# Rotary embedding: the first batch moved in two-row pieces, with sine and cosine tables of its own

## The chip, the cores and the metric

The kernel runs on one core of a Trainium2 chip. A core has five engines that run their own instruction streams: TensorE (PE, matrix products into PSUM), VectorE (DVE), ScalarE (ACT), GpSimd (POOL) and SyncE (SP, which only issues transfers and waits). Sixteen DMA engines move data between the device memory (HBM) and the core's on-chip memory (SBUF, 128 partitions). SP and ACT issue DMAs here, each into a queue of its own; both queues are served by the same sixteen DMA engines. Engines wait for each other through counters called semaphores; a DMA raises its semaphore by 16 when all its parts have landed.

The metric is device time in microseconds (us) for one execution, lower is better. It is given as the median of several executions. The profile is of one further execution, and its span runs from the first to the last instruction.

## The reference

```python
batch, seq, dim, num_heads = 16, 512, 1024, 16      # head_dim 64, half_dim 32
x = x.reshape(batch, seq, num_heads, head_dim)
x1, x2 = x[..., :half_dim], x[..., half_dim:]
cos, sin = cos[None, :, None, :], sin[None, :, None, :]      # each [seq, 32]
rotated = concatenate([x1 * cos - x2 * sin, x1 * sin + x2 * cos], axis=-1)   # float32
```

Every row of 1024 numbers (one position of one batch) is split into 16 heads of 64, and each head's two halves are rotated by the angle of the position. The input has 33.6 MB, the output as much; the tables have 64 KB each.

## The kernel before

**Tiles.** A batch has 512 rows of 4 KB. Four consecutive rows of one batch make a partition's share in a tile of a single batch (`R1 = 4`), eight rows in a tile of two batches (`R2 = 8`, 64 partitions for each batch). There are ten tiles: batches 0 and 1 alone, then six pairs, then batches 14 and 15 alone (line 41). The text calls them t0 to t9: t0 and t1 are the first two batches, t2 to t7 the pairs, t8 and t9 the last two batches. The buffer `x_sb` is a ring of 40 row slots in each partition, so that t0 to t5 are loaded without waiting for anything, and t6 to t9 take slots over from tiles that have been stored. A tile of a single batch moves in pieces of 16 KB for each partition, a pair in pieces of 32 KB.

**One row slot.** A row slot `u` (64 in all) holds one row in each partition, 128 x 1024 numbers. DVE multiplies it by the cosine into PSUM (`mul`, line 293), POOL multiplies the row with its halves swapped by the sine, one half negated, into `t2_sb`, a ring of six (line 257); one row in eight of a pair is multiplied by DVE instead (line 286). The sum is formed in one of two ways: DVE adds both into `x_sb` (`comb`, line 304), or, for the slots marked in `PE2` (three of eight, away from both ends), PE adds the sine product onto PSUM through an identity matrix (line 224) and ACT copies the result into `x_sb` (line 191). PSUM has three slots for this, so DVE's `mul(u)` waits until slot `u - 3` has been added and read.

**Tables.** `stage` receives cosine and sine in the order of a single batch (four rows for each partition). DVE copies the cosine into PSUM (`c1_ps`, line 264), ACT makes the negated and the plain sine (`s1_sb`, lines 182 and 183). For pairs PE rearranges the tables with the matrix `pick` (line 208) into `pair_ps`, and ACT makes `s2_sb` from it (lines 186 and 187).

**Order.** All orders are written out by hand. ACT issues the load of t0, the two table loads, then the loads of t1 to t5 (lines 153 and 174); then it makes `pick` and the sine tables, and after that walks over the slots. In that walk it also issues the later loads, after slot 17, 25 and 33: t6 once the stores of t0 and t1 have landed (`sem_out[0]`), t7 once that of t2 has, t8 and t9 once that of t3 has (lines 192 to 195). ACT is a single stream, so while it waits for such a store, its next copy (line 191) waits too. SP walks over the slots and issues a tile's store when the tile's last slot is finished (line 161). POOL starts when the sine table and t0 are there (lines 250 to 255). Everything goes out with semaphores, and nothing is decided at run time.

Of the kernel before, what the change touches and what calls it, by code (L numbers as in the profile page):

```python
# [6 lines left out]
def bass_split_heads_rope_kernel(  # L7
# [16 lines left out]
    batch, seq, dim = x.shape  # L24
    H = int(num_heads)
    HD = dim // H
    HALF = HD // 2
    P = 128
    R1 = seq // P
    R2 = 2 * R1  # L30
    assert R1 * P == seq and R1 == 4 and batch % 2 == 0

    fp32 = mybir.dt.float32
# [3 lines left out]
    COPY = mybir.ActivationFunctionType.Copy  # L37
# [3 lines left out]
    tiles = [(b, R1 if b in singles else R2) for b in range(batch) if b in singles or b % 2 == 0]  # L41
# [26 lines left out]
    with ExitStack() as stack:  # L68
        x_sb = stack.enter_context(nc.sbuf_tensor([P, RING, H, 2, HALF], fp32))
        t2_sb = stack.enter_context(nc.sbuf_tensor([P, NT2, H, 2, HALF], fp32))  # L70
        stage = stack.enter_context(nc.sbuf_tensor([P, 2, R1 * HALF], fp32))
        s1_sb = stack.enter_context(nc.sbuf_tensor([P, R1, 2, HALF], fp32))
        s2_sb = stack.enter_context(nc.sbuf_tensor([P, R2, 2, HALF], fp32))
        ident = stack.enter_context(nc.sbuf_tensor([P, P], fp32))
# [2 lines left out]
        tab_ps = stack.enter_context(nc.psum_tensor([P, BANK], fp32))  # L77
# [5 lines left out]
        sem_cos = stack.enter_context(nc.semaphore("cos"))  # L83
# [9 lines left out]
        sem_e = stack.enter_context(nc.semaphore("pe"))  # L93
        sem_g = stack.enter_context(nc.semaphore("pick"))
        sem_t = stack.enter_context(nc.semaphore("pairs"))
        sem_a = stack.enter_context(nc.semaphore("act"))

        c1_ps = tab_ps[:, 0:R1 * HALF].rearrange("p (r d) -> p r d", d=HALF)
        v_ps = tab_ps[:, R1 * HALF:R1 * HALF + HD].rearrange("p (t d) -> p t d", d=HALF)

        def c_of(t, r):
            return c1_ps[:, r, :] if tiles[t][1] == R1 else pair_ps[:, r // R1, 0, r % R1, :]

        def s_of(t, r):
            return s1_sb[:, r] if tiles[t][1] == R1 else s2_sb[:, r]

        x1 = x.rearrange("b (s r) d -> b s (r d)", r=R1)
        o1 = out.rearrange("b (s r) h d -> b s (r h d)", r=R1)
# [4 lines left out]
        def in_dram(single, pairs, t):  # L113
            b, n = tiles[t]
            return single[b] if n == R1 else pairs[:, b:b + 2, :]

        def in_sbuf(t):
            b, n = tiles[t]
            k = b * R1 % RING
            return x_sb[:, k:k + n].rearrange("p n h t d -> p (n h t d)")  # L120
# [26 lines left out]

        def stores_of(k):

            return sum(b * R1 // R2 == k for b, _ in tiles)  # L150

        def load(eng, t):
            eng.dma_start(in_sbuf(t), in_dram(x1, x2, t)).then_inc(sem_in[t], 16)  # L153

        def on_sync(sp):
            for u in range(NU):
                t, r, k = where(u)
                if r == tiles[t][1] - 1:
                    wait_added(sp, u)
                    k = u // R2  # L160
                    sp.dma_start(in_dram(o1, o2, t), in_sbuf(t)).then_inc(sem_out[k] if k < EARLY else sem_rest, 16)
            sp.wait_ge(sem_rest, 16 * sum(stores_of(k) for k in range(EARLY, NU // R2)))

        def on_scalar(ae):
            later = {}
            for t, (b, n) in enumerate(tiles):
                if b * R1 + n <= RING:
                    load(ae, t)
                else:

                    later.setdefault((b * R1 - RING) // R2 * R2 + R2 - 1 + LAG, []).append(t)
                if t == 0:
                    for i, (table, sem) in enumerate(((cos, sem_cos), (sin, sem_sin))):
                        ae.dma_start(stage[:, i, :], table.rearrange("(s r) d -> s (r d)", r=R1)).then_inc(sem, 16)  # L174

            ae.wait_ge(sem_i, 2)
            ae.activation(  # L177
                pick[:], ident[:].rearrange("q (s k) -> q k s", k=2)[:, :, :, None].broadcast_to([P, 2, P // 2, 2]), COPY
            ).then_inc(sem_g, 1)
            ae.wait_ge(sem_sin, 16)  # L180
            sv = stage[:, 1, :].rearrange("s (r d) -> s r d", d=HALF)
            ae.activation(s1_sb[:, :, 0, :], sv, COPY, scale=-1.0)  # L182
            ae.activation(s1_sb[:, :, 1, :], sv, COPY).then_inc(sem_s, 1)  # L183
            ae.wait_ge(sem_t, 2)
            s2 = s2_sb[:].rearrange("p (k r) t d -> p k r t d", r=R1)
            ae.activation(s2[:, :, :, 0, :], pair_ps[:, :, 1, :, :], COPY, scale=-1.0)  # L186
            ae.activation(s2[:, :, :, 1, :], pair_ps[:, :, 1, :, :], COPY).then_inc(sem_s, 1)  # L187
            for u in range(NU):
                if PE2[u]:
                    ae.wait_ge(sem_e, n_pe[u])  # L190
                    ae.activation(xs[:, u % RING, :], t1_ps[:, u % NT1, :], COPY).then_inc(sem_a, 1)  # L191
                for t in later.get(u, ()):
                    k = (tiles[t][0] * R1 - RING) // R2
                    ae.wait_ge(sem_out[k], 16 * stores_of(k))
                    load(ae, t)
# [38 lines left out]
        def on_gpsimd(pl):  # L234
            pl.memset(ident[:], 1.0).then_inc(sem_i, 1)  # L235
            pl.wait_ge(sem_i, 1)
            pl.affine_select(  # L237
                out=ident[:],
                in_=ident[:],
                compare_op=mybir.AluOpType.is_equal,  # L240
                fill=0.0,
                base=0,
                pattern=[[-1, P]],
                channel_multiplier=1,
            ).then_inc(sem_i, 1)
            for u in range(NU):
                if V2[u]:
                    continue
                t, r, k = where(u)
                if (t, r) == (0, 0):  # L250
                    pl.wait_ge(sem_s, 1)
                if (t, r) == (2, 0):
                    pl.wait_ge(sem_s, 2)
                if r == 0:
                    pl.wait_ge(sem_in[t], 16)
                wait_t2_free(pl, u)
                pl.tensor_tensor(  # L257
                    t2_sb[:, u % NT2, :, :, :], swapped(k), over_heads(s_of(t, r)), mult
                ).then_inc(sem_p, 1)

        def on_vector(ve):
            ve.memset(zero[:], 0.0).then_inc(sem_z, 1)  # L262
            ve.wait_ge(sem_cos, 16)
            ve.tensor_copy(c1_ps, stage[:, 0, :].rearrange("s (r d) -> s r d", d=HALF)).then_inc(sem_c, 1)  # L264
            ve.wait_ge(sem_c, 1)
            ve.wait_ge(sem_w, NT1 * EH)

            def pair_tables():
                ve.wait_ge(sem_s, 2)
                row = pair_ps[:, V_ROW // R1, 1, V_ROW % R1, :]  # L270
                ve.tensor_scalar_mul(v_ps[:, 0, :], row, -1.0).then_inc(sem_c, 1)
                ve.tensor_copy(v_ps[:, 1, :], row).then_inc(sem_c, 1)

            first_v = V2.index(True)

            def mul(u):
                t, r, k = where(u)
                if r == 0:
                    ve.wait_ge(sem_in[t], 16)
                if (t, r) == (2, 0):  # L280
                    pair_tables()
                if u == first_v:
                    ve.wait_ge(sem_c, 3)
                if V2[u]:
                    wait_t2_free(ve, u)
                    ve.tensor_tensor(t2_sb[:, u % NT2, :, :, :], swapped(k), over_heads(v_ps), mult)  # L286
                if u >= NT1:
                    v = u - NT1
                    if PE2[v]:
                        ve.wait_ge(sem_a, n_pe[v])  # L290
                    else:
                        ve.wait_ge(sem_v, n_comb[v])
                ve.tensor_tensor(  # L293
                    t1_ps[:, u % NT1, :].rearrange("p (h d) -> p h d", d=HALF),
                    x_sb[:, k, :, :, :].rearrange("p h t d -> p (h t) d"),
                    c_of(t, r)[:, None, :].broadcast_to([P, 2 * H, HALF]),
                    mult,
                ).then_inc(sem_m, 1)

            def comb(u):  # L300
                t, r, k = where(u)
                ve.wait_ge(sem_m, u + 1)
                ve.wait_ge(sem_p, n_pool[u])  # L303
                ve.tensor_tensor(  # L304
                    xs[:, k, :],
                    t1_ps[:, u % NT1, :],
                    t2_sb[:, u % NT2, :, :, :].rearrange("p h t d -> p (h t d)"),
                    add,
                ).then_inc(sem_v, 1)

            for u in range(NU + LEAD):
                if u < NU:
                    mul(u)
                if u >= LEAD and not PE2[u - LEAD]:
                    comb(u - LEAD)
# [39 lines left out]
```

## Time and profile before

| | |
|---|---|
| time, median of 3 runs | 161.21 us (161.02 to 161.35) |
| profiled execution, span | 160.3 us |
| DMA: packets, bytes, mean rate | 3170, 67.26 MB, 419 GB/s |
| busy share of the span: POOL, DVE | 84%, 81% |
| busy share of the span: PE, ACT | 45%, 15% |
| POOL's first multiply | starts at 9.85 us |
| issue to landing, load of t0 | 8.0 us |
| issue to landing, store of t0 | 18.6 us |

The time of the profiled execution is known by its span alone; the span is 0.9 us under the median of the runs. A line of a timeline has the start in us, the length in us, the engine, the source line, the operation, what it writes and reads, how often it ran, and in square brackets how long the engine had been idle before it and what ended that. "ACTq" and "SPq" are DMA issues on ACT and SP. The chain is the work that ended last, followed back from the end: start, length, what. In the DMA view a queue's line has its packets, MB, and its packets' share of the time of 16 DMA engines; q10 is the queue of ACT (the loads) and q1 that of SP (the stores). The row "DMA" of the page gives the busy share of the DMA engines in 40 equal slices of the span, in tenths.

### The profile page before, as it was taken

How to read it: one execution, taken by the hardware profiler on the slowest of the kernel's cores; microseconds unless marked ns; L12 is line 12 of the kernel's file. 1: busy time of each engine (PE TensorE's matmuls, PEld its weight loads, DVE VectorE, ACT ScalarE, POOL GpSimd, SP SyncE). 2: the span in 40 equal slices, each digit the busy share in tenths (PEclk: the TensorE clock that was granted, in tenths of full speed). 3: DMA queues.
4: the chain of work that ended last, by engine and by line, in shares of the span. 5: the costliest groups of instructions: out<-in, count | busy, mean ns of one | idle time of the engine just before them, and what ended most of it. 6: DMA issues, size and time to landing. Idle time of an engine off the chain costs nothing.

```text
span 160.3 us, 522 instructions
## 1 busy us (share of the span) xinstructions
PE 72.8 (45%) x94; PEld 24.0 (15%) x94; DVE 130.3 (81%) x117; ACT 24.4 (15%) x27; POOL 134.9 (84%) x64
## 2 busy tenths in 40 slices
PE   6050004478357936660847105489458435850000
PEld 1020002022202211210221002022202111220000
DVE  0069998599989999996999709899889999999500
ACT  0420000203120222022012010201220402040000
POOL 1059999999999999999999999699999999289400
PEclk9955555557755587689687965555555977699555
DMA  5999999999999999999999999999999999999896
GB/s 147 409 441 474 409 450 409 425 429 429 446 429 458 417 411 466 409 433 401 450 433 425 425 409 458 409 433 433 411 429 462 441 417 401 450 441 441 376 450 294
DMA packets 3170, 67.26 MB, mean 419 GB/s; under 512 B 352, under 2 KB 608, under 8 KB 608
## 3 DMA queue, kind: packets, MB, share of 16 engines
q10 hardware_dynamic: 1728, 33.69, 49.6%
q1 hardware_dynamic: 1440, 33.56, 48.9%
q14 instruction: 2, 0.02, 0.0%
HBM read 33.69 MB, written 33.55 MB: 419 GB/s over the span
## 4 chain that ended last, share of the span: by engine, by line
DMA 60%; POOL 13%; DVE 8%; PE 7%; issue 3%; ACT 2%; ACTq 1%; DVEq 0%
DMA x_sb<-in_x_dram 41%; DMA out_dram<-x_sb 18%; POOL t_sb L257 13%; PE t_ps L224 7%; DVE t_ps L293 5%; DVE x_sb L304 3%; ACT x_sb L191 2%; ACTq L153 1%; ACTq L174 1%; DVE t_sb L286 0%; DVEq L303 0%
## 5 line engine op out<-in xcount | busy, mean ns | idle before, releaser
L257 POOL TENSOR_TENSOR t_sb<-x_sb,s_sb 128x1024 f32<-128x1024 f32 x58 | 134.2, 2346 | 14.8 <-ACT s_sb L183 8.5
L224 PE MATMUL t_ps<-t_sb,ident 128*128 128x512 f32 x84 | 68.0, 957 | 63.0 <-DVE t_ps L293 39.2
L293 DVE TENSOR_TENSOR t_ps<-x_sb,pair_ps 128x1024 f32<-128x1024 f32 x48 | 57.7, 1223 | 9.9 <-ACT x_sb L191 9.8
L304 DVE TENSOR_TENSOR x_sb<-t_ps,t_sb 128x1024 f32<-128x1024 f32 x43 | 52.4, 1218 | 2.6 <-POOL t_sb L257 2.6
L224 PEld LDWEIGHTS t_ps<-t_sb,ident 128*128 128x128 f32 x84 | 22.1, 290 | 108.9 <-DVE t_ps L293 74.6
L191 ACT ACTIVATE x_sb<-t_ps 128x1024 f32<-128x1024 f32 x21 | 21.5, 1023 | 109.9 <-PE t_ps L224 96.9
L293 DVE TENSOR_TENSOR t_ps<-x_sb,tab_ps 128x1024 f32<-128x1024 f32 x16 | 19.3, 1222 | 0.1
L286 DVE TENSOR_TENSOR t_sb<-x_sb,tab_ps 128x1024 f32<-128x1024 f32 x6 | 7.3, 1213 | 0.0
L264 DVE COPY tab_ps<-stage 128x128 f32<-128x128 f32 x1 | 0.3, 294 | 7.8 <-DMA stage<-in_cos_dram 7.8
L208 PE MATMUL pair_ps<-stage,pick 128*128 128x256 f32 x4 | 2.0, 667 | 5.4 <-DMA stage<-in_sin_dram 5.4
L201 PE MATMUL t_ps<-zero 128*128 128x512 bf16 x6 | 2.7, 627 | 1.3 <-DVE zero L262 1.3
L208 PEld LDWEIGHTS pair_ps<-stage,pick 128*128 128x128 f32 x4 | 1.2, 324 | 6.4 <-issue 6.3
L177 ACT ACT_TABLE_LOAD x1 | 1.3, 1283 | 5.5 <-issue 5.5
L201 PEld LDWEIGHTS t_ps<-zero 128*128 128x128 bf16 x6 | 0.7, 136 | 2.4 <-DVE zero L262 1.2
L262 DVE MEMSET zero<- 128x256 uint32 x1 | 0.3, 272 | 0.9 <-PEq L337 0.9
L186 ACT ACTIVATE s_sb<-pair_ps 128x256 f32<-128x256 f32 x1 | 0.4, 383 | 1.7 <-PE pair_ps L208 1.7
L182 ACT ACTIVATE s_sb<-stage 128x128 f32<-128x128 f32 x1 | 0.3, 309 | 2.1 <-DMA stage<-in_sin_dram 2.1
L235 POOL MEMSET ident<- 128x128 f32 x1 | 0.2, 204 | 0.3 <-POOLq L337 0.3
L177 ACT ACTIVATE pick<-ident 128x256 f32<-128x256 f32 x1 | 0.4, 416 | 0.0
L187 ACT ACTIVATE s_sb<-pair_ps 128x256 f32<-128x256 f32 x1 | 0.4, 379 | 0.0
L237 POOL TENSOR_SCALAR_AFFINE_SELECT ident<-ident 128x128 f32<-128x128 f32 x1 | 0.3, 292 | 0.1
L337 POOL MEMSET const-float32-0.0<- 128x1 f32 x1 | 0.1, 98 | 0.3 <-issue 0.3
(6 smaller groups left out, 1.0 us busy)
## 6 DMA issues: line engine op xcount, KB each, us to landing
x_sb<-in_x_dram ACTq DMA_DIRECT2D x6, 4096.0 KB, 38.0
out_dram<-x_sb SPq DMA_DIRECT2D x6, 4096.0 KB, 25.0
x_sb<-in_x_dram ACTq DMA_DIRECT2D x4, 2048.0 KB, 22.6
out_dram<-x_sb SPq DMA_DIRECT2D x4, 2048.0 KB, 15.2
stage<-in_cos_dram ACTq DMA_DIRECT2D x1, 64.0 KB, 7.8
stage<-in_sin_dram ACTq DMA_DIRECT2D x1, 64.0 KB, 7.5
```

The costliest lines, as they stand in the source:

```text
L153: eng.dma_start(in_sbuf(t), in_dram(x1, x2, t)).then_inc(sem_in[t], 16)
L174: ae.dma_start(stage[:, i, :], table.rearrange("(s r) d -> s (r d)", r=R1)).then_inc(sem, 16)
L177: ae.activation(pick[:], ident[:].rearrange("q (s k) -> q k s", k=2)[:, :, :, None].broadcast_to([P, 2, P // 2, 2]), COPY).then_inc(sem_g, 1)
L186: ae.activation(s2[:, :, :, 0, :], pair_ps[:, :, 1, :, :], COPY, scale=-1.0)
L191: ae.activation(xs[:, u % RING, :], t1_ps[:, u % NT1, :], COPY).then_inc(sem_a, 1)
L201: pe.matmul(t1_ps[:, k, b * BANK:(b + 1) * BANK], zero[:, 0:P], zero[:], start=True, stop=True).then_inc(sem_w, 1)
L208: pe.matmul(pair_ps[:, k].rearrange("p c r d -> p (c r d)"), pick[:, k].rearrange("q s b -> q (s b)"), stage[:].rearrange("q c f -> q (c f)"),
L224: ins = pe.matmul(t1_ps[:, u % NT1, b * BANK:(b + 1) * BANK], ident[:], t2[:, b * BANK:(b + 1) * BANK], start=False, stop=True, skip_group ...
L257: pl.tensor_tensor(t2_sb[:, u % NT2, :, :, :], swapped(k), over_heads(s_of(t, r)), mult).then_inc(sem_p, 1)
L286: ve.tensor_tensor(t2_sb[:, u % NT2, :, :, :], swapped(k), over_heads(v_ps), mult)
L293: ve.tensor_tensor(t1_ps[:, u % NT1, :].rearrange("p (h d) -> p h d", d=HALF), x_sb[:, k, :, :, :].rearrange("p h t d -> p (h t) d"), c_of ...
L304: ve.tensor_tensor(xs[:, k, :], t1_ps[:, u % NT1, :], t2_sb[:, u % NT2, :, :, :].rearrange("p h t d -> p (h t d)"), add,).then_inc(sem_v, 1)
```

## The change

For t0 alone the assignment of rows to partitions changes. Batch 0's 512 rows are taken as 256 pieces of two rows. Partition `4g + i` (g from 0 to 31, i from 0 to 3) holds pieces `32i + g` and `128 + 32i + g`. The load is two DMAs, one for each half of the batch, with 8 KB for each partition, and the store likewise. The sine and cosine rows must stand in the same order, so t0 has tables of its own: SP loads them, after it has waited for the identity, by four DMAs of 256 bytes for each partition into `stage0` (`sem_f`); ACT makes `s0_sb` and DVE `c0_ps` of them. The old table loads into `stage` stay, for t1, t8, t9 and the pairs, but ACT issues them after the load of t1 instead of before it. The copy into `c1_ps` moves to DVE's first slot of t1. The counts of the semaphores follow: `sem_s` and `sem_c` have one step more, the wait for t0's load is for 32, and `sem_out[0]` counts three stores.

```diff
+        stage0 = stack.enter_context(nc.sbuf_tensor([P, 2, 2, R1 // 2 * HALF], fp32))
+        s0_sb = stack.enter_context(nc.sbuf_tensor([P, R1, 2, HALF], fp32))
...
+        R0 = R1 // 2
+
+        def swept(rows_of, half):
+            n = seq // 2
+            return rows_of[half * n:(half + 1) * n].rearrange("(i g r) d -> g i (r d)", g=P // 4, r=R0)
...
         def stores_of(k):
-            return sum(b * R1 // R2 == k for b, _ in tiles)
+            return sum(b * R1 // R2 == k for b, _ in tiles) + (k == 0)
 
         def load(eng, t):
+            if t == 0:
+                for half in range(2):
+                    eng.dma_start(in_sbuf(0)[:, half * R0 * H * HD:(half + 1) * R0 * H * HD], swept(x[0], half)).then_inc(
+                        sem_in[0], 16
+                    )
+                return
             eng.dma_start(in_sbuf(t), in_dram(x1, x2, t)).then_inc(sem_in[t], 16)
 
         def on_sync(sp):
+            sp.wait_ge(sem_i, 2)
+            for half in range(2):
+                for i, table in enumerate((cos, sin)):
+                    sp.dma_start(stage0[:, i, half, :], swept(table, half)).then_inc(sem_f, 16)
             for u in range(NU):
...
                     k = u // R2
+                    if t == 0:
+                        o_rows = out[0].rearrange("s h d -> s (h d)")
+                        for half in range(2):
+                            sp.dma_start(
+                                swept(o_rows, half), in_sbuf(0)[:, half * R0 * H * HD:(half + 1) * R0 * H * HD]
+                            ).then_inc(sem_out[k], 16)
+                        continue
...
         def on_scalar(ae):
...
-                if t == 0:
+                if t == 1:
                     for i, (table, sem) in enumerate(((cos, sem_cos), (sin, sem_sin))):
                         ae.dma_start(stage[:, i, :], table.rearrange("(s r) d -> s (r d)", r=R1)).then_inc(sem, 16)
...
+            ae.wait_ge(sem_f, 64)
+            sv = stage0[:, 1].rearrange("s k (r d) -> s (k r) d", d=HALF)
+            ae.activation(s0_sb[:, :, 0, :], sv, COPY, scale=-1.0)
+            ae.activation(s0_sb[:, :, 1, :], sv, COPY).then_inc(sem_s, 1)
             ae.wait_ge(sem_sin, 16)
...
         def on_gpsimd(pl):
...
-                if (t, r) == (0, 0):
-                    pl.wait_ge(sem_s, 1)
-                if (t, r) == (2, 0):
-                    pl.wait_ge(sem_s, 2)
+                if t < 3 and r == 0:
+                    pl.wait_ge(sem_s, t + 1)
                 if r == 0:
-                    pl.wait_ge(sem_in[t], 16)
+                    pl.wait_ge(sem_in[t], 32 if t == 0 else 16)
...
         def on_vector(ve):
             ve.memset(zero[:], 0.0).then_inc(sem_z, 1)
-            ve.wait_ge(sem_cos, 16)
-            ve.tensor_copy(c1_ps, stage[:, 0, :].rearrange("s (r d) -> s r d", d=HALF)).then_inc(sem_c, 1)
+            ve.wait_ge(sem_f, 64)
+            ve.tensor_copy(c0_ps, stage0[:, 0].rearrange("s k (r d) -> s (k r) d", d=HALF)).then_inc(sem_c, 1)
...
+                if (t, r) == (1, 0):
+                    ve.wait_ge(sem_cos, 16)
+                    ve.tensor_copy(c1_ps, stage[:, 0, :].rearrange("s (r d) -> s r d", d=HALF)).then_inc(sem_c, 1)
+                    ve.wait_ge(sem_c, 2)
```

Left out are the semaphore's declaration, `c0_ps` and the branches of `c_of` and `s_of` that choose t0's tables, and the later counts of `sem_s` and `sem_c`, each raised by one.

More of the change, by code (lines that the diff above doesn't have):

```diff
@@ L95, in bass_split_heads_rope_kernel @@
         sem_t = stack.enter_context(nc.semaphore("pairs"))
+        sem_f = stack.enter_context(nc.semaphore("first"))
         sem_a = stack.enter_context(nc.semaphore("act"))
@@ L99, in bass_split_heads_rope_kernel @@
         v_ps = tab_ps[:, R1 * HALF:R1 * HALF + HD].rearrange("p (t d) -> p t d", d=HALF)
+        at = R1 * HALF + HD
+        c0_ps = tab_ps[:, at:at + R1 * HALF].rearrange("p (r d) -> p r d", d=HALF)
         def c_of(t, r):
+            if t == 0:
+                return c0_ps[:, r, :]
             return c1_ps[:, r, :] if tiles[t][1] == R1 else pair_ps[:, r // R1, 0, r % R1, :]
         def s_of(t, r):
+            if t == 0:
+                return s0_sb[:, r]
             return s1_sb[:, r] if tiles[t][1] == R1 else s2_sb[:, r]
+        R0 = R1 // 2
+        def swept(rows_of, half):
+            n = seq // 2
+            return rows_of[half * n:(half + 1) * n].rearrange("(i g r) d -> g i (r d)", g=P // 4, r=R0)
         x1 = x.rearrange("b (s r) d -> b s (r d)", r=R1)
@@ L148, in stores_of @@
         def stores_of(k):
-            return sum(b * R1 // R2 == k for b, _ in tiles)
+            return sum(b * R1 // R2 == k for b, _ in tiles) + (k == 0)
         def load(eng, t):
+            if t == 0:
+                for half in range(2):
[3 more added lines that the diff above has]
+                return
             eng.dma_start(in_sbuf(t), in_dram(x1, x2, t)).then_inc(sem_in[t], 16)
         def on_sync(sp):
+            sp.wait_ge(sem_i, 2)
+            for half in range(2):
+                for i, table in enumerate((cos, sin)):
+                    sp.dma_start(stage0[:, i, half, :], swept(table, half)).then_inc(sem_f, 16)
             for u in range(NU):
@@ L160, in on_sync @@
                     k = u // R2
+                    if t == 0:
+                        o_rows = out[0].rearrange("s h d -> s (h d)")
[4 more added lines that the diff above has]
+                        continue
                     sp.dma_start(in_dram(o1, o2, t), in_sbuf(t)).then_inc(sem_out[k] if k < EARLY else sem_rest, 16)
@@ L268, in pair_tables @@
             def pair_tables():
-                ve.wait_ge(sem_s, 2)
+                ve.wait_ge(sem_s, 3)
                 row = pair_ps[:, V_ROW // R1, 1, V_ROW % R1, :]
@@ L278, in mul @@
                 if r == 0:
-                    ve.wait_ge(sem_in[t], 16)
+                    ve.wait_ge(sem_in[t], 32 if t == 0 else 16)
+                if (t, r) == (1, 0):
+                    ve.wait_ge(sem_cos, 16)
+                    ve.tensor_copy(c1_ps, stage[:, 0, :].rearrange("s (r d) -> s r d", d=HALF)).then_inc(sem_c, 1)
+                    ve.wait_ge(sem_c, 2)
                 if (t, r) == (2, 0):
@@ L282, in mul @@
                 if u == first_v:
-                    ve.wait_ge(sem_c, 3)
+                    ve.wait_ge(sem_c, 4)
                 if V2[u]:
```

## The prediction

> **What bounds the kernel now.** I read the page's utilisation rows first, then the table of stretches, the DMA view of one stretch, the chain, and the timelines of ACT and DVE. I call the ten load tiles t0 to t9: t0 and t1 are the first two batches, t2 to t7 are pairs, t8 and t9 the last two batches. The page, rows of the span and of DMA:
>
> ```profile
> span 160.3 us, 522 instructions
> ...
> DMA  5999999999999999999999999999999999999896
> ...
> q10 hardware_dynamic: 1728, 33.69, 49.6%
> q1 hardware_dynamic: 1440, 33.56, 48.9%
> ```
>
> Loads (q10) and stores (q1) fill 98.5% of the 16 DMA engines. The packet records (start, length and size of each) say the same: first packet at 1.82 us, last end at 159.95, lengths summing to 157.9 us per engine. Only dead time, slow packets or fewer packets can be saved. Next, how two queues share an engine, from the DMA view of 24 to 38 us, when t0's store (16 KB packets) ran beside pair loads (32 KB packets):
>
> ```profile
> q10 hardware_dynamic: 134, 3.90, 65.5%
> q1 hardware_dynamic: 133, 2.06, 34.4%
> ```
>
> Equal packets, unequal bytes: the queues take turns by packet, so a queue with smaller packets is served more slowly. The turns are single packets: in the records t0's store packets begin at an even 8 per 0.9 us on the 16 engines. Third, the chain and the stalls (chain; ACT timeline; DVE timeline):
>
> ```profile
> 63.68 29.38 DMA out_dram<-x_sb
> 93.06 0.02 issue
> 93.08 0.33 ACTq L153
> 93.41 0.04 issue
> 93.45 47.51 DMA x_sb<-in_x_dram
> 140.96 0.07 issue
> 141.02 9.29 POOL t_sb L257 x4
> ```
>
> ```profile
> 85.64 1.02 ACT L191 ACTIVATE x_sb<-t_ps 128x1024 f32<-128x1024 f32 x1 [4.68 <-PE t_ps L224]
> 93.08 2.40 ACTq L153 DMA_DIRECT2D x_sb<-in_x_dram  x2
> 95.52 1.02 ACT L191 ACTIVATE x_sb<-t_ps 128x1024 f32<-128x1024 f32 x1 [8.86 <-issue]
> ```
>
> ```profile
> 96.58 1.23 DVE L293 TENSOR_TENSOR t_ps<-x_sb,pair_ps 128x1024 f32<-128x1024 f32 x1 [5.31 <-ACT x_sb L191]
> ```
>
> ACT issues the later loads only after the store that frees their slots: t8 and t9 wait for t3's store, landed at 93.06. ACT's next activation is queued behind that wait, and DVE then idles 5.31 us. So the landing of t3's store sets when computing goes on; from 96 us DVE is nearly unbroken to the end. The tail decides how much delay is free (SP timeline; DVE timeline):
>
> ```profile
> 135.58 16.46 SPq L161 DMA_DIRECT2D out_dram<-x_sb  x3
> ```
>
> ```profile
> 150.40 1.23 DVE x_sb L304
> ```
>
> Stores of t7, t8, t9 are issued at 135.58, 143.57 and 151.70 (same view, narrower windows). They are still queued: t6's store lands at 141.2 (119.57 + 21.6 in the issue view), t8's at 155.5.
>
> **The change, part by part.** Durations are of one packet on one engine: 32 KB 1.213 us, 16 KB 0.611, 512 B 0.027, a semaphore write 0.009. From the first two, 16 KB costs 0.602 plus 0.009 per packet, so 8 KB is estimated at 0.310.
>
> *DMA work.* t0's load and store become 16 packets of 8 KB per engine instead of 8 of 16 KB: 2 x 16 x 0.310 against 2 x 8 x 0.611, +0.14. Six more DMAs write semaphores: 6 x 0.009 = +0.05. SP's four table loads add 32 packets of 256 B per engine; no such size is in the trace, so between the 4 B row (0.009, +0.3) and twice the 512 B row (0.054, +1.7); by bytes 0.018, nearest the 512 B row, +0.58. Sum +0.77, from +0.5 to +1.9. Nothing hides it, since the engines are never free. The skill's page "DMA: Bandwidth & Descriptors" (Specifications) speaks against such pieces: below 512 B a transfer is a read-modify-write. No run here shows one; at twice the price the sum would be +1.4 (estimate from that page).
>
> *The order of t0.* The first 36 packets average 0.942 us, which is 36 x 0.331 / 16 = 0.75 us of excess. Whether reading along addresses removes it the trace cannot tell: from -0.75 to +0.75 (a second ragged start). I take 0, as the excess sits in each engine's first two packets and 8 KB packets also begin there.
>
> *Start of computing.* Before, POOL starts at 9.85, when sin has landed (9.24) and ACT has scaled it. After, t0 needs SP's four table loads. SP is free once the identity is done (1.08 + 0.29 us) and issues over about 4 x 0.46. Its 36 packets per engine then alternate with ACT's queue: some 14 of t0, 8 of t1 and their semaphores, then ACT's own 16 table packets, now behind t1. They are through when t1 is, at about 1.82 + 0.75 + 4.96 + 4.89 + 0.63 + 0.3 = 13.4, and land some 0.7 later. ACT's two table copies (0.6) put POOL's start at 14.7 and t0's store issue near 25.7 instead of 20.48, with 0.3 for DVE's second table copy, which now stands ahead of t1. The same page (Queues, rings and completion order) says an engine drains 9 to 17 descriptors before switching queue; then the tables would land with t0 near 9 us. By that rule the sum would still be 163.0, since the check by sum below holds for any start.
>
> *Stores early on.* The price is here. Before: t0's store runs 24.0 to 38.6 (8 turns of 1.213 + 0.611), t1's to 53.2; then t2's and t3's take 16 turns of 2.426, to 92.0, landed 1.06 later. After: issue 25.7 plus the 3.4 us that 20.48 to the first packet at 23.9 took gives 29.1. t0's store is now 16 turns of 1.213 + 0.310 = 24.4, to 53.5. In that time 16 load packets pass, so 3 of the up-front loads (t0 to t5) are left; they run out at 59.0 beside t1's store, which ends at 62.2. Check by sum: 1.82 + 0.75 + loads 4.96 + 4.89 + 4 x 9.70 + tables 1.0 + stores 4.96 + 4.89 = 62.1, whatever the start. ACT cannot issue t6's load until then (62.6, was 53.60); its first packet comes at 66.0. t2's store has 3.8 us alone (3.1 packets); the other 12.9 of t2 and t3 take 31.3, to 97.2. So t3's store lands 5.2 us later. Between ends: with tables and shares as before, 0.7; if t6's first packet needs 1.0 us (0.81 to 1.82, the first load) rather than 3.4, 7.7. I take 5.2, by the row of a queue joining a busy engine.
>
> *What is late next.* ACT's activation and DVE, hence SP's stores, move by 5.2: t7's to 140.8, t8's to 148.8. t9's load now ends near 134, so POOL's wait for it (DVE's last 1.08 us of idle) goes: t9's store at 151.70 - 1.08 + 5.2 = 155.8. Against that the DMA: t6's store really ends near 140.2, now 140.9. t7's first packet comes at 141.8 (1.0 after issue on an empty queue), 0.9 us idle; it ends at 151.5, t8's at 156.4; t9's starts at 156.8, ends at 161.7, and the span ends 0.4 later (as 159.95 to 160.34): 162.1, against 160.34. About 1.8 us: 0.8 is packets, the rest idle. The profiled execution is known by its span; the median of the runs, 161.21, is 0.87 above it. 162.1 + 0.87 = 163.0.
>
> The other edits: SP's wait for the identity delays nothing, as its first store is 20 us off; a third semaphore count on POOL and the c1 copy on DVE stand ahead of t1, whose tables land near 14; the scalings for t0 cost ACT 0.6, counted above.
>
> **The rivals.**
> *Hidden.* Stores late by less than about 3 us (t7's issue at 135.58 against 140.2 - 1.0, and t9's at 150.6 against 155.0 - 1.0) leave the engines no gap. ACT's issue of t9's load took 2.02 us where other single-tile issues took 0.34 to 0.66; with less queued it may shrink, and the 5.2 becomes 3.6. Then only packets are paid: 161.21 + 0.5 to 0.9 = 161.7 to 162.1. Against it: the sums above give more.
> *The sweep pays (not slower).* Reading t0 along addresses removes the 0.75 us of slow first packets. Place: 1.8 to 4 us. It decides only if the stores also stay under 3 us late and a table packet costs 0.027 or less: 161.21 + 0.77 - 0.75 = 161.2, or down to 160.7 with table packets at 0.009 and some turns better filled. For it: 36 packets at 0.942; against: the other 476 16 KB loads at 0.611 to 0.63 in the old order.
> *Tables overrun.* If SP's queue begins after 5 us, each table packet left when ACT's own are gone alternates with a 32 KB load, 1.213 us each. Four to eight left put the start 5 to 10 us further back; past the 5.2 already paid it goes to the end: 165.5 to 170. For it: the 3.4 us that a joining queue needed; against: that was behind 32 KB packets.
>
> **How the numbers follow.** Forecast (162.2 to 165.5, the top being stores 7.7 late: 155.8 + 2.5, then 6.3 to the end, plus 0.87) 0.55; hidden 0.15; the sweep pays 0.18; overrun 0.10; all else 0.02. A change under 0.2% (0.32 us) cannot be told from none here: the sweep case splits into 0.11 faster and 0.07 same, the rest is slower, 0.82. The range leaves out overrun and the lower half of the sweep case: 161.0 to 165.5; the likeliest case alone is 162.2 to 165.5.
>
> **What would show it.** POOL's first multiply near 14.7 (near 9.4 if the tables are not held up); t0's stores landing some 28 us after issue rather than 18.6; t6's load issued near 62.6, t8's near 98; DMA slices under 9 near 141 us; t9's store issued near 155.8. I am wrong if t8's load goes out before 96 us, or if the first 36 load packets run at full rate and the span ends by 161.

## The result and the profile after

The changed kernel takes 163.33 us (median of 4 runs, 162.97 to 164.18) against 161.28 for the kernel before (4 runs, 161.02 to 161.52): a ratio of 1.0131 with a 95% interval of 1.0109 to 1.0152. The forecast was 163.0. The profiled execution has a span of 161.9 us, before 160.3. Medians here and below are over all runs, while the ratios leave out the slow ones, those more than 1.5% above their kernel's fastest.

The page of the changed kernel, the same rows as before:

```profile
span 161.9 us, 533 instructions
...
DMA  4999999898997999999999999999999999799997
...
q10 hardware_dynamic: 1872, 33.69, 49.0%
q1 hardware_dynamic: 2160, 33.69, 48.7%
```

Of the slices inside the span, the 8th, 10th and 13th (8, 8 and 7) and the 35th (7), from 137.6 to 141.7 us, stand under the 9 that they had before. The row counts a packet whole in the slice in which it starts; by the packets' own starts and ends the engines are full in the first three, and 66% busy in the 35th. The table of stretches shows that gap (columns: stretch, its length, busy us of PE, PEld, DVE, ACT and POOL with the number of instructions, granted PE clock, DMA share, GB/s). Before, then after:

```profile
140.00:144.00 4.00, 2.36 (x5) 0.88 (x4) 4.00 (x5) 2.05 (x2) 2.98 (x2) 0.90 1.01 434
```

```profile
140.00:144.00 4.00, 2.34 (x3) 1.17 (x4) 3.63 (x4) 0.34 (x1) 4.00 (x3) 0.50 0.62 262
```

Nearly 40% of the DMA engines' time between 140 and 144 us is lost by this view, 1.36 of the 4 us by the packets' own starts and ends. This is the forecast gap: t6's store had been written and t7's had only just been issued. The store's time is in SP's timeline:

```profile
140.37 15.46 SPq L196 DMA_DIRECT2D out_dram<-x_sb  x3
```

The chain before the gap, from ACT's timeline of the changed kernel:

```profile
15.04 0.29 ACT L218 ACTIVATE s_sb<-stage 128x128 f32<-128x128 f32 x1
...
64.02 0.54 ACTq L177 DMA_DIRECT2D x_sb<-in_x_dram  x1
64.61 1.02 ACT L230 ACTIVATE x_sb<-t_ps 128x1024 f32<-128x1024 f32 x1 [4.91 <-DMA out_dram<-x_sb]
...
99.04 0.89 ACTq L177 DMA_DIRECT2D x_sb<-in_x_dram  x2
99.97 1.02 ACT L230 ACTIVATE x_sb<-t_ps 128x1024 f32<-128x1024 f32 x1 [6.54 <-DMA out_dram<-x_sb]
```

t6's load goes out at 64.02 (53.60 before) and those of t8 and t9 at 99.04 (93.08 before); each time ACT's next copy stands behind the wait for a store.

Summed over the packet records, as a mean of the 16 engines, the loss at the end of the last packet (161.43 against 159.95, so 1.49 us) has three parts. The first packet comes at 2.21 instead of 1.82 (+0.39). The packets' own time per engine is 158.12 instead of 157.92 (+0.20). The rest, in the main time with nothing to move, is 1.10 instead of 0.21 (+0.89): the gap of 1.36, less what the engines save by ending nearly together. The medians lie further apart, by 2.05 us; why is said behind the experiments.

### The profile page after: what moved, and what is told of

Read it like the earlier page. It is cut to its first block, busy times and chain, and to the rows that moved or that the text cites. A ratio compares the mean times of both kernels' runs of the same rounds, so it can differ in the third digit from the quotient of the medians.

```text
span 161.9 us, 533 instructions
## 1 busy us (share of the span) xinstructions
PE 72.4 (45%) x94; PEld 23.5 (14%) x94; DVE 130.3 (80%) x118; ACT 24.8 (15%) x29; POOL 134.8 (83%) x64
## 4 chain that ended last, share of the span: by engine, by line
DMA 38%; POOL 19%; PE 14%; DVE 10%; issue 8%; ACT 4%; ACTq 1%; POOLq 0%; DVEq 0%
DMA out_dram<-x_sb 34%; POOL t_sb L294 19%; PE t_ps L263 14%; DVE t_ps L334 6%; DMA x_sb<-in_x_dram 5%; ACT x_sb L230 4%; DVE x_sb L345 4%; ACTq L177 1%; DVE t_sb L327 1%; ACTq L173 0%; POOLq L292 0%; DVEq L331 0%
## 5 line engine op out<-in xcount | busy, mean ns | idle before, releaser
L294 POOL TENSOR_TENSOR t_sb<-x_sb,s_sb 128x1024 f32<-128x1024 f32 x58 | 134.1, 2355 | 14.7 <-ACT s_sb L218 14.0
L263 PE MATMUL t_ps<-t_sb,ident 128*128 128x512 f32 x84 | 67.7, 955 | 62.2 <-DVE t_ps L334 40.4
L263 PEld LDWEIGHTS t_ps<-t_sb,ident 128*128 128x128 f32 x84 | 21.6, 283 | 108.2 <-DVE t_ps L334 69.1
```

The costliest lines, as they stand in the source:

```text
L263: ins = pe.matmul(t1_ps[:, u % NT1, b * BANK:(b + 1) * BANK], ident[:], t2[:, b * BANK:(b + 1) * BANK], start=False, stop=True, skip_group ...
L294: pl.tensor_tensor(t2_sb[:, u % NT2, :, :, :], swapped(k), over_heads(s_of(t, r)), mult).then_inc(sem_p, 1)
```

## The experiments

All twelve kernels were timed in turn with the kernel before, in three rounds (its medians there: 161.30, 161.36 and 161.28); "ratio" is to that, with its 95% interval. A "spread" below is the time between the first and the last of the 16 DMA engines to report one store as written, from the landing records; the "last spread" is that of t9's store. "Slow packets" is the time that packets took beyond the median of their size, as a mean of the 16 engines. All these, and every time inside a kernel, are of its one profiled execution. The packet records don't name the engine.

**The gate moved in the changed kernel.**

```diff
-    LAG = 10
+    LAG = 14
```

> The changed kernel with one number altered: ACT issues the later loads four slots later in its walk (after slots 21, 29 and 37 instead of 17, 25 and 33). Gate theory (late stores hold ACT, ACT holds DVE, and the DMA engines run dry at the tail): ACT finds the stores landed, DVE's waits for ACT shrink from 9.4 us to under 4, t7's store is issued before 138 us instead of 140.4, the 1.4 us of missing DMA work at 140 to 144 us is gone, and the time falls by 0.8 to 1.3 us to 162.0 to 162.6. What stays against the kernel before, about 0.6 us, is the later first packet (2.2 against 1.8) and the added packets. Packet theory (small and swept packets cost it all): time unchanged, 163.3. Start theory (computing begins 5.6 us later and that goes to the end): unchanged too, 163.3, with t9's store still issued near 155.5.

Measured: 162.39 us (12 runs), ratio 1.0072 (1.0045 to 1.0098). The interval lies below the changed kernel's. DVE's waits for ACT fall to 3.3 us, and the last three stores start early (SP's timeline, then the table of stretches):

```profile
133.54 17.84 SPq L196 DMA_DIRECT2D out_dram<-x_sb  x3
```

```profile
140.00:144.00 4.00, 1.95 (x4) 0.68 (x4) 3.55 (x4) 1.27 (x2) 4.00 (x3) 1.00 1.06 459
```

POOL starts as late as in the changed kernel (15.54 and 15.42) and the gap is gone all the same. So ACT's wait, and not the late start alone, made the gap, and it cost some 0.9 us (0.94 between the medians). The start theory, by which the time stays at 163.3, falls.

**The same in the kernel before.** The same edit of `LAG`.

> The kernel before with ACT's later loads issued after slots 21, 29 and 37. Gate theory: DVE's 5.3 us wait near 91 us goes and the stores are issued earlier, but the DMA engines were never short of work in the kernel before, so the time stays within 0.3 us of it, 161.1 to 161.6. Rival (the gate costs the kernel before something too): 160.0 to 160.8.

Measured: 161.34 us (12 runs), ratio 0.9998 (0.9985 to 1.0010). DVE's waits for ACT fall from 9.8 to 3.6 us and nothing comes of it. A stall on two engines is worth nothing while the DMA engines have work.

This kernel also prices what is left of the change without the gate, since both now have the late one: 162.39 against 161.34. In the profiled executions (162.69 and 161.30) the first packet comes 0.40 us later, the packets take 158.13 instead of 157.45 us per engine (+0.68), and the rest is 0.42 instead of 0.19 (+0.22).

**The store's pieces alone.** The kernel before, with only this, and the count of `sem_out[0]` one store higher:

```diff
+                    if t == 0:
+                        w = R1 // 2 * H * HD
+                        for half in range(2):
+                            sp.dma_start(
+                                o1[0][:, half * w:(half + 1) * w], in_sbuf(0)[:, half * w:(half + 1) * w]
+                            ).then_inc(sem_out[k], 16)
+                        continue
```

> The kernel before, with one thing of the change: t0's store as two DMAs of 8 KB for each partition, in the old order of rows. No added tables, start of computing as before (POOL 9.85). Gate theory: the store of t0 lands near 49 instead of 39, t6's load is issued near 62.7 instead of 53.6, t8's near 98.5 instead of 93.1, and the time is 162.0 to 162.8, most of the change's loss without its tables and its order. Packet theory: 0.1 us more, 161.4. Start theory: 161.3, as the start is unchanged.

Measured: 164.96 us (6 runs; the profiled one 163.80), ratio 1.0195 (1.0143 to 1.0246), more than the whole change. The steps up to ACT came as expected (SP's stores of t0, then ACT):

```profile
20.19 0.85 SPq L164 DMA_DIRECT2D out_dram<-x_sb  x2
```

```profile
62.97 0.54 ACTq L153 DMA_DIRECT2D x_sb<-in_x_dram  x1
63.56 1.02 ACT L198 ACTIVATE x_sb<-t_ps 128x1024 f32<-128x1024 f32 x1 [9.72 <-DMA out_dram<-x_sb]
...
97.97 0.88 ACTq L153 DMA_DIRECT2D x_sb<-in_x_dram  x2
```

But t9's store is issued at 152.72, early enough, and there is no gap at 140. The end is late for another reason. The first DMA engine reports t9's store at 158.93 (159.11 in the kernel before), the last one at 162.35 (160.31): a spread of 3.4 us instead of 1.2. Fourteen engines report by 159.53; one at 160.98 and the last run behind the others. The records have a few slow packets that fit: one at 66.6 us takes 1.17 us too long, and the spread goes from 0.9 at t1's store to 2.2 at t2's; some between 120 and 128 take up to 0.6 too long, and it goes from 2.2 to 3.6. The gate theory didn't have this, and its number was missed.

**Store's pieces, with the gate moved.** The last kernel with `LAG = 14`.

> The kernel before with t0's store in two DMAs of 8 KB for each partition and ACT's later loads issued after slots 21, 29 and 37. In the profiled execution of the split store alone no gap stood at the tail; one DMA engine was 3.4 us behind the others instead. Gate theory: that straggling follows from the loads running dry near 60 us and rejoining all at once, which the later gate does not change in time (t6's load still near 63), so it may stay; what the gate itself costs goes: 161.4 to 163. Straggler theory (the split store's loss is the one engine, not the wait on ACT): 164 to 165 as with the split store alone, spread of the last landings over 2 us.

Measured: 164.91 us (6 runs), ratio 1.0209 (1.0176 to 1.0242). With the late gate in both, the split store is the only difference between this and the 161.34 above. The tables of stretches at the end, first without it, then with it:

```profile
156.00:159.00 3.00, 0.00 (x0) 0.00 (x0) 0.00 (x0) 0.00 (x0) 0.00 (x0) 0.50 0.88 377
159.00:161.00 2.00, 0.00 (x0) 0.00 (x0) 0.00 (x0) 0.00 (x0) 0.00 (x0) 0.50 0.00 0
```

```profile
156.00:159.00 3.00, 0.00 (x0) 0.00 (x0) 0.00 (x0) 0.00 (x0) 0.00 (x0) 0.50 0.91 388
159.00:161.00 2.00, 0.00 (x0) 0.00 (x0) 0.00 (x0) 0.00 (x0) 0.00 (x0) 0.50 0.25 107
161.00:164.00 3.00, 0.00 (x0) 0.00 (x0) 0.00 (x0) 0.00 (x0) 0.00 (x0) 0.50 0.06 27
```

A share of 0.25, and then of 0.06, is a few engines finishing alone; the spread of the last store is 4.5 us. So in the kernel before a small store at 20 us costs some 3.6 us with either gate, and in the trace nearly all of it stands as engines that straggle. Small pieces alone don't decide it: the changed kernel stores the same pieces at 26 us, and with the late gate takes 162.39.

**The late start alone.** The kernel before, with one line moved:

```diff
-                if t == 0:
+                if t == 1:
                     for i, (table, sem) in enumerate(((cos, sem_cos), (sin, sem_sin))):
```

> The kernel before, with one line moved: ACT issues the two table loads after t1's load instead of before it. Nothing else. POOL starts near 14.6 instead of 9.85. Gate theory: all stores start 4.7 us later at the old packet size, t6's load goes out near 58.3, t8's near 97.5 (4.5 later than 93.1), and the time is 161.4 to 162.4: a late start alone does about as much as the small packets alone, and the two do not add. Start theory: all of the change's loss, 163. Packet theory: 161.3, no change.

Measured: 162.05 us (12 runs), ratio 1.0036 (1.0013 to 1.0058). POOL starts at 14.52; t6's load goes out at 59.45 and t8's at 98.17; the packets fill 3.77 of the 4 us from 136 and 3.80 of those from 152, so there are two small gaps like the one of the changed kernel, 0.43 us in all. A start 4.7 us later costs 0.8 between the medians, and not 4.7. That the gaps are what costs it isn't shown: in the profiled execution (161.77) the engines end closer together (a last spread of 0.2), which makes up for them.

**The start made early again.** The changed kernel, with t0's tables on ACT's queue:

```diff
-            sp.wait_ge(sem_i, 2)
-            for half in range(2):
-                for i, table in enumerate((cos, sin)):
-                    sp.dma_start(stage0[:, i, half, :], swept(table, half)).then_inc(sem_f, 16)
...
+                if t == 0:
+                    for half in range(2):
+                        for i, table in enumerate((cos, sin)):
+                            ae.dma_start(stage0[:, i, half, :], swept(table, half)).then_inc(sem_f, 16)
```

> The changed kernel with t0's own four table loads issued by ACT right behind t0's load instead of by SP, so that they no longer alternate with t1's packets. POOL starts near 10 instead of 15.4. Gate theory: t6's load still goes out near 63 and t8's near 98.5, because the store of t0 is still in 8 KB packets, and the time stays at 162.8 to 163.4. Start theory: most of the loss goes, 161.8 to 162.1. Packet theory: unchanged, 163.3.

Measured: 164.50 us (6 runs), ratio 1.0178 (1.0137 to 1.0218). POOL starts at 11.23 and the kernel is slower, not faster. t6's load goes out at 64.38 and t8's at 99.46, 1.0 to 1.4 us later than expected, and the time lies above what the gate theory gave; the spread of t2's store is 3.4 us, and slow packets add 1.16 us per engine between 60 and 100 (0.04 in the changed kernel).

**The early start, with the gate moved.** The last kernel with `LAG = 14`.

> The changed kernel with t0's tables issued by ACT behind t0's load, and with ACT's later loads after slots 21, 29 and 37. Gate theory: computing starts near 11.3 as with the tables on ACT alone, nothing holds ACT, no gap at the tail; what is left is the first packet at 2.2 to 2.3 and 0.6 us of table packets: 162.0 to 162.6, at most a tenth or two under the changed kernel with the late gate alone. Start theory: the early start is worth a us or more on top: 161.4 or less.

Measured: 164.40 us (6 runs), ratio 1.0194 (1.0168 to 1.0220), last spread 2.5 us. Its last store is issued at 149.81, so nothing but the DMA engines sets the end. Both theories missed. Why an earlier start makes slow packets and stragglers is open.

**The load's pieces alone.** The kernel before, with t0's load as two DMAs of 8 KB for each partition in the old order (and the waits for it at 32):

```diff
+            if t == 0:
+                w = R1 // 2 * H * HD
+                for half in range(2):
+                    eng.dma_start(in_sbuf(0)[:, half * w:(half + 1) * w], x1[0][:, half * w:(half + 1) * w]).then_inc(
+                        sem_in[0], 16
+                    )
+                return
```

> The kernel before with t0's load alone as two DMAs of 8 KB for each partition, old order of rows, store unchanged. Gate theory: the packets cost 0.1 us, nothing waits: 161.2 to 161.6. Packet theory: part of the change's loss, 161.8 or more. It also gives the start: with the old order the first packet at 1.8 as before and the first 36 packets slow, against 2.2 and a smaller excess in the changed kernel; if the first packet is at 2.2 here too, it is the two DMAs and not the order of rows that delays it.

Measured: 161.83 us (12 runs), ratio 1.0038 (1.0013 to 1.0063), with a last spread of 1.5 us. That is over the gate theory's 161.6 and at the edge of the packet theory's 161.8, so it doesn't decide between them. The first packet comes at 1.81. So the 2.21 of the changed kernel isn't from the two DMAs.

**The order of rows undone.** The changed kernel, with:

```diff
         def swept(rows_of, half):
-            n = seq // 2
-            return rows_of[half * n:(half + 1) * n].rearrange("(i g r) d -> g i (r d)", g=P // 4, r=R0)
+            return rows_of.rearrange("(s k r) d -> s k (r d)", k=2, r=R0)[:, half, :]
```

> The changed kernel with the order of rows undone: partition s holds rows 4s to 4s + 3 of batch 0 again, still in two pieces of two rows for load, store and tables, and all else as changed. My working (the order is worth nothing by itself): the time stays near 163.3; the first packet may come at 1.8 instead of 2.2 since ACT's issue is shorter, which would give 162.9 to 163.3. Sweep theory (reading along addresses helps): 163.8 or more, with the first 36 packets slow again.

Measured: 162.45 us (9 runs), ratio 1.0092 (1.0063 to 1.0121). The first packet is back at 1.82, and t8's load goes out at 98.27 instead of 99.04, although POOL starts later, at 16.31. The sweep theory (163.8 or more) falls, and the working's 162.9 to 163.3 was missed too. The order seems to cost something by itself: its issue on ACT takes 0.61 us instead of 0.38, and the first packet comes 0.39 later. In the first 10 us the slow packets cost 0.64 us per engine in the changed kernel and 0.68 in this one, so the sweep saves next to nothing there. The interval overlaps the changed kernel's, so 0.9 us as the order's price isn't firm.

**Do engines straggle because the load queue runs dry?** In the kernel with the small store and the late gate the last up-front load packet ends at 61.9 us, and t6's first one starts at 67.7. In the first kernel below, which is that one, t6's load is cut in two halves of row slots and the first is issued when t0's store has landed, so that the load queue never empties (the second half and the counts are left out of the diff); in the second, the kernel before, with the late gate, gets a dry spell without any small packet.

```diff
+                if u == R2 - 1 + 10:
+                    w = R2 // 2 * H * HD
+                    ae.wait_ge(sem_o0, 32)
+                    ae.dma_start(in_sbuf(6)[:, 0:w], in_dram(x1, x2, 6)[:, :, 0:w]).then_inc(sem_in[6], 16)
```

> The split store with the late gate, and with t6's load in two halves of four row slots: the first half is issued as soon as t0's store has landed, the second when t1's has. The load queue then has work without a break. Rejoin theory (the loads run dry near 60 us, and when they start again near 66 some DMA engines lose a packet's time, 1.2 us at a go, which the last landing pays): the landings of t2's store on the 16 engines lie within 1.6 us instead of 2.9, no packet near 66 takes twice its time, and the time falls by 2 to 3.5 us, to 161.4 to 162.8. Packet theory (small store packets themselves): still 164 to 165.

Measured: 164.23 us (6 runs), ratio 1.0140 (1.0086 to 1.0194). The six runs stand in pairs: 162.1 and 162.2, 164.2 and 164.2, 166.2 and 166.3. The profiled one is of the first pair; there t2's store has a spread of 0.8 and the last store 1.4, as the rejoin theory wants. Of the other four there is no trace. The theory is not carried by the times: all six have the same edit, and they differ by 2 us and more.

```diff
-                    later.setdefault((b * R1 - RING) // R2 * R2 + R2 - 1 + LAG, []).append(t)
+                    later.setdefault((b * R1 - RING) // R2 * R2 + R2 - 1 + LAG + (4 if t == 6 else 0), []).append(t)
```

> The kernel before with the late gate, and t6's load held until after slot 25, so that the load queue runs dry near 70 us for about 3 us, with no small packet anywhere. Rejoin theory: packets near 73 to 76 take up to twice their time on some engines, the landings of the stores spread over 2 us or more from then on (0.9 to 1.1 without it), and the time rises by 1 to 3 us, to 162.3 to 164.3. Packet theory: spread about 1 us, 161.2 to 162.0.

Measured: 163.11 us (4 runs), ratio 1.0112 (1.0098 to 1.0126). The spread goes from 1.0 at t2's store to 3.9 at t3's, and two packets at 74 us take twice their time. The load queue is dry from 70.8 to 73.3 there, so in this execution stragglers come with a dry spell and no small packet. The time itself can't be put down to them, since the held-back load also made t9's store late (155.18).

Third, the same halved load in the changed kernel with the late gate.

> The changed kernel with the late gate and t6's load in two halves, the first issued when t0's store has landed (near 55). Gate and rejoin theories together: no gap at the tail, no straggling engine, what is left is the first packet at 2.2 and 0.6 us of table packets: 161.7 to 162.2, against 162.4 with the late gate alone. If it is 162.4 or more, the rejoin costs nothing where computing starts late.

Measured: 164.92 us (6 runs; the profiled one 163.94), ratio 1.0225 (1.0194 to 1.0256), 2.5 us slower than with the late gate alone. The edit does only half of what it was meant to: t6's first half goes out at 58.63, and the load queue is still dry from 59.4 to 62.8 us. The spread is 1.6 us at t2's store and grows at t3's (3.2), near 91 us, with no dry spell there.

The traces of all kernels together leave a link, not a cause: in the nine in which the load queue runs dry for 2.4 us or more the spread at t3's store is 2.0 to 3.9 us, in the other five 0.9 to 2.1. But the end doesn't follow it (last spreads from 0.2 to 4.5 in the nine). So the rejoin theory by itself doesn't explain the stragglers. What decides which engine loses a packet's time, and when, stays open. No kernel tried was faster than the kernel before.

## Why the prediction was right, and where it was not

*The gate.* The chain named in the prediction is what the trace shows: t0's store in small packets, t6's load held back, t3's store landing late, ACT, DVE, and a dry tail. t6's load was put at 62.6 and came at 64.02, its first packet 4.3 us after that where the working took 3.4, and t3's store was put 5.2 us late and landed 6.0 late (99.02 for 93.06). t7's store was put at 140.8 (140.37), t9's at 155.8 (155.49), the span at 162.1 (161.9). Moving the gate took some 0.9 us back, which shows the chain to be the cause of that much, a little under half of the 2.05.

*Part of the hidden rival.* It had said that ACT's issue of t9's load would shrink from 2.02 us. It did, to 0.51, and so ACT's next copy moved by 4.45 us where t3's store moved by 6.0. That wasn't enough to close the gap.

*The start of computing.* 14.7 was forecast, 15.42 measured. SP's first packets came near 5.2 us, 3.8 after the issue, and the 128 of its first table all started within 0.6 us; from 6 to 13 us the records then count 217 load packets against 189 of the tables. In the kernel with the order undone there is no such burst, and between 9 and 12 us loads and table packets come one to one (24 and 24, 27 and 27, 25 and 25 per us). That is the working's alternation. The rule of the Trainium skill's page "DMA: Bandwidth & Descriptors" (Queues, rings and completion order), typically 9 to 17 descriptors before a switch, leaves room for that first burst, but by it the tables would have landed near 9 us (the working's estimate); they landed near 14.8. In the changed kernel, up to t6's load, the start mattered as little as the working said: it went out at 64.02 with POOL's start at 15.42, and at 64.38 with it at 11.23.

*Packets.* The sum was +0.77, and between the two profiled executions +0.20 came. The sum itself was right: a 256-byte packet took 0.018 us, an 8 KB packet 0.309, and counted at the median of each size the packets cost +0.74. But slow packets, which the sum left as they were, fell from 1.73 to 1.20 us per engine, and that is in part the choice of execution. Later runs have 1.4 us between span and time, also those of the kernel before, so its profiled execution with a span of 160.3 stands for a run of some 161.7 (an estimate), above its median. The kernel before with the late gate is as fast and was profiled in a run at its median (161.30); there slow packets cost 1.27, and against it the packets of the changed kernel are at +0.67. The read-modify-write below 512 B, which the same page's Specifications tell of, doesn't show in the price of these packets: 0.018 is what the bytes and the 0.009 per packet give.

*The first packet.* Not in the working at all: +0.39 us, which comes with the reordered load and goes when its order is undone; 0.23 of it is the longer issue on ACT. Between the profiled executions the three parts are +0.39, +0.20 and +0.89, where the working had 0, +0.77 and some +1.0. The total was met partly by luck: the missing first packet stands against a kernel before that was profiled in a slow-packet execution.

*The own time of the profiled execution.* The working put 0.87 us around the span. In this and all later runs 1.4 us lies around it (163.31 against 161.9; 162.69 against 161.3), so the sum from span to time was 0.5 short there. The span itself was put 0.2 too high, and the forecast came out 0.3 low.

*What it missed altogether.* The working took the sixteen DMA engines as one, with equal work and one end. In the changed kernel that went well: the gap near 140 lets the engines that are behind catch up, and the spread falls from 1.3 us at t6's store to 0.2 at t7's. Where there is no gap the slowest engine decides, and the check "the sum is the same for any start" says nothing about it. By that check the kernel with the early start should have taken 163; it took 164.5.

## What to carry to other kernels

Where two DMA queues share engines packet by packet, halving the packets of one transfer halves what it moves for each packet of the other queue (t0's store took 22.5 us from first to last packet instead of 14.1): look at what waits for that transfer, and what is queued behind that wait, before the bytes. A stall costs nothing as long as the bounding engines have work, so the tail is where to work out whether a delay is free. And when the DMA engines are the bound, the slowest one of them ends the kernel (163.47 where the first was done at 158.93): compare the first and the last engine's landing, not the mean share.

## What was not expected of the hardware

Equal work didn't end at equal times. With a 2 MB store in 8 KB packets at 20 us, and everything else the same (both with the late gate), the first of 16 engines reported the last store at the same time (158.93 for 158.86) and the last engine 3.6 us later (163.47 for 159.85). The records have single packets of 32 KB there that took up to 2.43 us instead of 1.21, between 66 and 69 us, and the spread grows at the stores that follow.

A load described in three dimensions (32 by 4 by 8 KB) took ACT 0.61 us to issue, and its first packet came at 2.21; as many bytes in two dimensions took 0.38, with the first packet at 1.82. Whether the form of the description or the order of the addresses delays the packet, no run separates.
